# Turning half of the values back to front through DRAM instead of multiplying by reversed activations

## The chip, the cores and the metric

The kernel runs on one core of a Trainium2 chip. The metric is the device time of one execution in microseconds (us), taken as the median over several runs. The engines are named as the profile names them: PE is TensorE (matrix products, with PEld for loading the stationary operand), DVE is VectorE, ACT is ScalarE, POOL is GpSimd, SP is SyncE. ACT, POOL and SP can start DMA transfers; an issue is listed as ACTq, POOLq or SPq.

## The reference, cut to what matters

Two decoder layers act on 256 tokens of width 2048, all in float32. The change lies in the first mixer of the first layer, in its second half, a gated linear recurrence of eight heads of width 128 called `hgrn2`:

```python
def mixer_ab(h, w_in, ...):
    u, v, q, f, i, g = jnp.split(h @ w_in, cuts, axis=-1)     # each 256 x 1024
    ...
    y_b = hgrn2(q, f, i, g, lower_bound, o_gain)

def hgrn2(q, f_logit, i, g, lower_bound, o_gain):
    ...
    k = (1.0 - lb) * jax.nn.sigmoid(-fl)
    vc = chunks(i)                                            # the values
    ...
        o_intra = jnp.einsum('bhts,bhsv->bhtv', scores, v_c)
        new_state = ... + jnp.einsum('bhsk,bhsv->bhkv', k_c * jnp.exp(G_end - G), v_c)
```

What is computed for the change is `i`, the values: the normalized input times a 2048 x 1024 matrix. The kernel sums over tokens in two blocks of 128, and it needs the second block of values with its tokens in reverse order (token 255 first).

## The kernel before

**Tiling.** Activations lie feature-major: 16 tiles `a` of 128 features, each with the high part and the low part of 256 tokens. Every weight piece is 128 x 1024 floats (512 KB). It goes through a fixed pipeline: SP issues its load into `w` (L195, five buffers), ACT rounds it to `wh` (L182, three buffers), DVE makes the rest `wl` (L183, three buffers), and PE multiplies with three products for each pair (high by high, high by low, low by high). PE reads a piece for about 2.6 us.

**Loops.** `project` makes one head's query from two pieces (L301). `project_tok` makes 512 columns of values for both token blocks from eight pieces (L325 to L327), with two accumulators, one for each block. `project_four` (L344 to L346) makes 512 gate columns. The loop over heads runs `project` for heads 0 to 7; `values` runs ahead of head 4 (values for heads 0 to 3) and ahead of head 7 (for heads 4 to 7). After head 7 comes `project_four` for the output gate.

**The reversed block before.** In `project_tok`, POOL copies both parts of each activation tile with the second block's tokens in reverse (L316, tile `ar`), and the second block's products use that copy as their stationary operand, so the values come out reversed. Each token's scale `Rt` has to be reversed too; the function `mirror` makes the reversed scales `Rr` on DVE, once. `values` then lets ACT scale both accumulators into `itok` (L798).

**Order of the work.** The recurrence of each head, `hgrn`, is a generator that is advanced one step by each `tick()`, that is, once for each weight piece. On ACT it copies decay levels (`E`, L729) that alternate with products on DVE (`kq`, L733), moves scores (`s128` L754, `st` L756, `s1` L765), and makes the next head's decay (`lf`, L695). On PE it makes the scores (L743, L751, L714) and the output (L773 to L775: `st0` and `s128` times the first block `itok[:, 0]`, `s1` times the reversed second block `itok[:, 1]`). The output step waits until `values` has entered its `itok` in the list `itoks` and two further ticks have passed. The framework's scheduler turns all of this into one fixed sequence for each engine. Every engine works its sequence from the front, and an instruction that waits holds up all behind it on that engine; that holds for a DMA issue too.

## Time and profile before

| | |
|---|---|
| median of 3 runs | 2175.03 us (2174.26 to 2176.19) |
| the profiled execution's own time | 2173.92 us |
| its span in the profile | 2172.1 us |
| PE busy | 2164.0 us, 100% of the span |
| DVE, ACT, POOL busy | 1601.1 us, 1313.6 us, 472.3 us |
| `project_tok` for the values | from 116 us to 184 us of the span |
| POOL's copies `ar<-a` | 32, together 19.6 us |

PE's work is fixed by the products, so the time is PE's busy time and the few microseconds in which PE waits. A change of anything else shows in the time only where it makes such a wait longer or shorter. The lines of the profile that carry this stand in the prediction.

### The profile page before, as it was taken

The numbers are of one execution on the slowest core, as the hardware profiler recorded it, in microseconds if no ns is written. First come the engines' busy times: TensorE is split into PE (matmuls) and PEld (weight loads), VectorE is DVE, ScalarE is ACT, GpSimd is POOL, SyncE is SP. The second block draws the span as 40 slices with busy tenths as digits, with TensorE's granted clock in tenths as the row PEclk, the third lists the DMA queues.
The fourth block names the chain that finished last, engine by engine and source line by source line (L and its number), as shares of the span: only waits on it lengthen the run. The fifth ranks groups of instructions, "written<-read, shape, count | busy, mean of one in ns | idle before, by whom it ended". The sixth has DMA issues, their size and how long they took to land.

```text
span 2172.1 us, 32509 instructions
## 1 busy us (share of the span) xinstructions
PE 2164.0 (100%) x10874; PEld 1900.8 (88%) x10874; DVE 1601.1 (74%) x2286; ACT 1313.6 (60%) x1951; POOL 472.3 (22%) x865
## 2 busy tenths in 40 slices
PE   9999999999999999999999999999999999999999
PEld 8988888888888888888888888888888888888888
DVE  7788768777567757776987887877777577667766
ACT  7678766665556545654666556666666466456642
POOL 1252221212012002111233443212211012011202
PEclk9999999999999999999999999999999999999999
DMA  8655677777676767776777766787777677666866
GB/s 311 209 160 177 209 238 222 240 233 236 210 228 206 235 209 219 226 237 206 241 230 229 238 207 209 221 246 222 230 227 242 198 232 217 228 215 204 251 212 192
DMA packets 492617, 483.55 MB, mean 223 GB/s; under 512 B 115137, under 2 KB 460369, under 8 KB 492321
## 3 DMA queue, kind: packets, MB, share of 16 engines
q1 hardware_dynamic: 465888, 453.27, 66.2%
q0 software_dynamic: 24832, 25.92, 5.1%
q10 hardware_dynamic: 1728, 2.28, 0.3%
q8 instruction: 85, 1.39, 0.3%
q14 instruction: 84, 0.68, 0.1%
HBM read 435.18 MB, written 2.11 MB: 201 GB/s over the span
## 4 chain that ended last, share of the span: by engine, by line
PE 94%; DVE 2%; ACT 2%; issue 1%; DMA 1%; POOL 0%; SPq 0%; ACTq 0%; DVEq 0%
PE pm L344 26%; PE pm L345 26%; PE pm L346 26%; PE pm L325 4%; PE pm L326 4%; PE pm L327 4%; PE pm L233 1%; PE pm L301 1%; ACT wh L182 1%; DVE wl L183 1%; DMA pt<-ptmp 1%; PE pm L257 1%; DVE kq L733 0%; ACT E L729 0%; DVE st L762 0%
## 5 line engine op out<-in xcount | busy, mean ns | idle before, releaser
L183 DVE TENSOR_TENSOR wl<-w,wh 128x1024 fp32r<-128x1024 f32 (+1 forms) x820 | 990.9, 1218 | 448.7 <-ACT wh L182 437.0
L182 ACT ACTIVATE wh<-w 128x1024 fp32r<-128x1024 f32 (+1 forms) x820 | 856.0, 1049 | 608.8 <-PE pm L346 447.7
L344 PE MATMUL pm<-wh,a 128*128 128x512 f32 x1728 | 655.9, 380 | 0.0
L345 PE MATMUL pm<-wl,a 128*128 128x512 f32 x1728 | 655.3, 379 | 0.3 <-DVE wl L183 0.3
L346 PE MATMUL pm<-wh,a 128*128 128x512 f32 x1728 | 654.9, 379 | 0.0
L364 POOL DMA_DIRECT2D zt<-tmp x413 | 223.5, 549 | 1134.6 <-DVE tmp L357 1022.6
L345 PEld LDWEIGHTS pm<-wl,a 128*128 128x128 f32 x1728 | 326.6, 189 | 47.4 <-DVE wl L183 1.4
L346 PEld LDWEIGHTS pm<-wh,a 128*128 128x128 f32 x1728 | 326.6, 189 | 46.2
L344 PEld LDWEIGHTS pm<-wh,a 128*128 128x128 f32 x1728 | 326.5, 189 | 46.2
L344 PE MATMUL pm<-wh,hid 128*128 128x512 f32 x688 | 260.8, 379 | 0.0
L345 PE MATMUL pm<-wl,hid 128*128 128x512 f32 x688 | 260.8, 379 | 0.0
L346 PE MATMUL pm<-wh,hid 128*128 128x512 f32 x688 | 260.8, 379 | 0.0
L326 PE MATMUL pm<-wl,a 128*128 128x512 f32 x416 | 158.1, 380 | 2.3 <-DVE wl L183 2.3
L325 PE MATMUL pm<-wh,a 128*128 128x512 f32 x416 | 158.7, 381 | 0.0
L327 PE MATMUL pm<-wh,a 128*128 128x512 f32 x416 | 157.8, 379 | 0.0
L345 PEld LDWEIGHTS pm<-wl,hid 128*128 128x128 f32 x688 | 130.0, 189 | 18.5
L346 PEld LDWEIGHTS pm<-wh,hid 128*128 128x128 f32 x688 | 130.0, 189 | 18.5
L344 PEld LDWEIGHTS pm<-wh,hid 128*128 128x128 f32 x688 | 130.0, 189 | 18.4
L1238 ACT ACTIVATE conv<-zt,pp 128x256 f32<-128x256 f32 x176 | 95.9, 590 | 70.6 <-DMA zt<-tmp 62.5
L364 POOL DMA_DIRECT2D turn<-tmp x160 | 86.9, 551 | 224.4 <-DVE tmp L357 129.6
L1239 DVE SCALAR_TENSOR_TENSOR conv<-zt,pp,conv 128x255 f32<-128x255 f32 x176 | 80.2, 479 | 54.4 <-ACT conv L1238 35.4
L357 DVE STREAM_TRANSPOSE tmp<-z 128x512 f32<-128x512 f32 x120 | 97.8, 851 | 7.1 <-ACT z L1224 5.1
(252 smaller groups left out, 2245.2 us busy)
## 6 DMA issues: line engine op xcount, KB each, us to landing
w<-in_w_up SPq DMA_DIRECT2D x352, 512.0 KB, 5.0
w<-in_w_dn SPq DMA_DIRECT2D x176, 512.0 KB, 5.0
w<-in_w_cqkv SPq DMA_DIRECT2D x96, 512.0 KB, 4.6
w<-in_w_abo SPq DMA_DIRECT2D x32, 512.0 KB, 4.9
w<-in_w_cg SPq DMA_DIRECT2D x32, 512.0 KB, 5.3
w<-in_w_co SPq DMA_DIRECT2D x32, 512.0 KB, 4.9
zt<-tmp SPq DMA_DIRECT2D x414, 32.0 KB, 2.6
zt<-tmp POOLq DMA_DIRECT2D x413, 32.0 KB, 2.4
```

The source lines that it names most:

```text
L182: r = deep["wh"] = SC.activation(wh, w, AF.Copy)
L183: deep["wl"] = V.tensor_tensor(wl, w, wh.bitcast(F32), ALU.subtract)
L325: PE.matmul(to_two(ps[T]), ah, h, start=k + i == 0, stop=False)
L326: PE.matmul(to_two(ps[T]), ah, l, start=False, stop=False)
L327: deep["last"] = PE.matmul(to_two(ps[T]), al, h, start=False, stop=k + i == KT - 1)
L344: PE.matmul(to_rows(ps[T]), ah, h, start=not begun and k + i == ks[0], stop=False)
L345: PE.matmul(to_rows(ps[T]), ah, l, start=False, stop=False)
L346: deep["mm"] = deep["last"] = PE.matmul(to_rows(ps[T]), al, h, start=False, stop=not more and k + i == ks[-1] + 1)
L357: V.transpose(tmp.rearrange("p (b m i t) -> p b m i t", b=4, m=4, t=2)[:, :, :, :, T], src(T).rearrange("p (m b j) -> p b m j", m=4, b=4))
L364: queues[(a + b) % len(queues)].dma_start(dst[BLK * b:BLK * (b + 1), :, a * n:(a + 1) * n], tmp[BLK * a:BLK * (a + 1), b * 4 * n:(b + 1) * ...
L1238: held(SC.activation(c, z, AF.Identity, bias=pp[:, cb:cb + 1], scale=w(2)))
L1239: V.scalar_tensor_tensor(c[:, 1:], z[:, :S - 1], w(1), c[:, 1:], ALU.mult, ALU.add)
```

## The change

The reversed copies on POOL, the reversed scales and the function `mirror` go. The second block's values come out in natural order. ACT scales them into a tile `late`, and a new generator `flip` takes them to `itok[:, 1]` by three DMAs, all issued on ACT: SBUF to a DRAM tile, that DRAM tile to a second one with the 128 rows read from the last to the first, and the second DRAM tile to SBUF. Each moves 256 KB (128 rows of 2 KB). `flip` issues one for each tick, and each needs the one before to have landed. `itoks` gets its entry when the third one is issued.

```diff
@@ mixes()
                 for m in both:
                     next(m, None)
                 yield
-            yield from mirror()
-
-        Rr = hp.tile([P, LANE], F32, tag="Rr", name="Rr")[:, 0:2]
-
-        def mirror():
-            yield
-            r = hp.tile([P, 512], F32, tag="junk", name=nm("junk"), bufs=1)
-            ra, rb = (r[:, i * BLK:(i + 1) * BLK] for i in range(2))
-            held(V.tensor_copy(ra, Rt[:, 1:2].to_broadcast([P, BLK])), "wl")
-            V.tensor_copy(Rr[:, 0:1], Rt[:, 0:1])
-            V.transpose(rb, ra)
-            V.transpose(ra, view(rb, BLK - 1, (-1, BLK)))
-            for a in range(4):
-                V.tensor_copy(Rr[BLK * (3 - a):BLK * (4 - a), 1:2], ra[BLK * a:BLK * (a + 1), 0:1])
@@ mixer_ab()
+        def flip(itok, late, r, f):
+            SC.dma_start(r, late)
+            yield
+            SC.dma_start(bass.AP(f.tensor, f.offset, [[S, 2], [512, P], [1, S]]),
+                         bass.AP(r.tensor, r.offset + (P - 1) * 512, [[S, 2], [-512, P], [1, S]]))
+            yield
+            SC.dma_start(itok[:, 1], f)
+            itoks.append((itok, steps[0]))
+
         def values(j):
-            ps = project_tok(w_i[j], norm, lambda: hp.tile([P, 512], F32R, tag="ar", name=nm("ar"), bufs=3))
+            ps = project_tok(w_i[j], norm)
             itok = hp.tile([P, 2, 512], F32, tag="tok", name=nm("itok"), bufs=2)
-            for T in range(2):
-                SC.activation(cols2(itok[:, T]), of_two(ps[T]), AF.Copy, scale=Rr[:, T:T + 1])
-            itoks.append((itok, steps[0]))
+            late = hp.tile([P, 512], F32, tag="ar", name=nm("late"), bufs=1)
+            SC.activation(cols2(late), of_two(ps[1]), AF.Copy, scale=Rt[:, 1:2])
+            SC.activation(cols2(itok[:, 0]), of_two(ps[0]), AF.Copy, scale=Rt[:, 0:1])
+            start(flip(itok, late, *rowsd[j]))
 
         silu = []
+        dp = es.enter_context(tc.tile_pool(name="da", bufs=1, space=bass.MemoryType.DRAM))
+        rowsd = [[dp.tile([P, 512], F32, tag=f"rd{i}{n}", name=f"rd{i}{n}") for n in range(2)] for i in range(2)]
...
             if h in (4, 7):
-                values(len(itoks))
+                values(h // 7)
```

The scheduler's sequences stay what they were except between the first `values` and the first pieces of the output gate, on PE, DVE, ACT and POOL; SP's sequence is the same. Three places of that stretch follow. The lines of the changed kernel are smaller by 15 there (L714 is L729 of before) and by 3 from `gated` on. The number at the end of a name is the program's own for that buffer, and it differs between the two kernels for the same piece.

First, ACT behind the first `values`. Before, both `itok` copies are followed by three weight pieces (`wh`) with the recurrence's work between them:

```order
L798 ACTIVATE itok_267_1644<-pm_218_1331,Rr_544 128x512
L798 ACTIVATE itok_267_1644<-pm_219_1332,Rr_544 128x512
L729 ACTIVATE E_252_1548<-kq_178_997 128x128 x2
L182 ACTIVATE wh_284_1785<-w_283_1784 128x1024
L754 ACTIVATE s128_271_1675<-px_270_1649 128x128
L756 ACTIVATE st1_974<-px_270_1649 64x64 x2
L695 ACTIVATE lf_206_1232<-lf_206_1232,gm_545 128x256
L182 ACTIVATE wh_289_1834<-w_288_1833 128x1024
L729 ACTIVATE E_277_1730<-kq_183_1033 128x128 x2
L182 ACTIVATE wh_297_1917<-w_296_1916 128x1024
L765 ACTIVATE s1_272_1684<-st1_974 128x128
```

The piece `wh_284` feeds the first half of head 5's query and `wh_289` its second half. In the changed kernel these two are `wh_275` and `wh_281`, and behind `itok`, `late` and one pair of `E` copies ACT's sequence is this:

```order
L780 DMA rd00_986<-late_259_1617 128x512
L739 ACTIVATE s128_263_1649<-px_262_1623 128x128
L741 ACTIVATE st1_973<-px_262_1623 64x64 x2
L182 ACTIVATE wh_275_1754<-w_274_1753 128x1024
L714 ACTIVATE E_269_1705<-kq_182_1029 128x128 x2
L680 ACTIVATE lf_205_1228<-lf_205_1228,gm_544 128x256
L782 DMA rd01_987<-rd00_986 2x128x256
L750 ACTIVATE s1_264_1658<-st1_973 128x128
L714 ACTIVATE E_269_1705<-kq_182_1029 128x128 x2
L836 ACTIVATE kq_206_1229<-pm_261_1622,gm_544 128x128 x2
L182 ACTIVATE wh_281_1810<-w_280_1809 128x1024
L785 DMA itok_258_1616<-rd01_987 128x512
```

The second half's piece, which stood ahead of the copy `s1`, now stands behind it, behind two pairs of copies and behind the second transfer; the third transfer follows it.

Second, PE in head 5's query, where the output step of head 0 stands. Before, the step stands ahead of that query, in one piece:

```order
L301 MATMUL pm_269_1648<-a_58_378,wh_279_1739 128x256 x2
L301 MATMUL pm_269_1648<-a_58_378,wl_280_1740 128x256
L773 MATMUL px_282_1771<-itok_267_1644,st0_973 128x128
L774 MATMUL px_282_1771<-itok_267_1644,s128_240_1486 128x128
L775 MATMUL px_282_1771<-itok_267_1644,s1_246_1511 128x128
L301 MATMUL pm_281_1770<-a_13_116,wh_284_1785 128x256 x2
L301 MATMUL pm_281_1770<-a_13_116,wl_285_1786 128x256
```

In the changed kernel it stands after the first half of the query, and its last product, which reads the reversed block, some rows further on:

```order
L301 MATMUL pm_273_1746<-a_38_256,wl_276_1755 128x256
L758 MATMUL px_277_1783<-itok_258_1616,st0_972 128x128
L759 MATMUL px_277_1783<-itok_258_1616,s128_240_1486 128x128
L301 MATMUL pm_273_1746<-a_39_290,wh_281_1810 128x256 x2
L301 MATMUL pm_273_1746<-a_39_290,wl_282_1811 128x256
L301 MATMUL pm_273_1746<-a_40_293,wh_281_1810 128x256 x2
L301 MATMUL pm_273_1746<-a_40_293,wl_282_1811 128x256
L301 MATMUL pm_273_1746<-a_44_315,wh_281_1810 128x256 x2
L760 MATMUL px_277_1783<-itok_258_1616,s1_241_1495 128x128
L301 MATMUL pm_273_1746<-a_44_315,wl_282_1811 128x256
```

PE's product L760 now waits for the third transfer, in the middle of the second half; the product L301 with `wl_282` ahead of it waits for that piece.

Third, ACT behind the second `values`, at the end of head 7's query. Before, the second piece of the output gate is `wh_375`:

```order
L182 ACTIVATE wh_370_2476<-w_369_2475 128x1024
L781 ACTIVATE px_355_2343,sos_972<-o_174_985,Rt_89_514 128x128
L729 ACTIVATE E_348_2310<-kq_221_1334 128x128 x2
L695 ACTIVATE lf_227_1373<-lf_227_1373,gm_545 128x256
L182 ACTIVATE wh_375_2507<-w_374_2506 128x1024
L99 ACTIVATE sos_972<-rm_359_2386 128x8
```

In the changed kernel that piece is `wh_360`. The second transfer (L782) stands two rows ahead of this excerpt:

```order
L714 ACTIVATE E_333_2265<-kq_220_1330 128x128
L99 ACTIVATE sos_971<-sos_971 128x8
L714 ACTIVATE E_333_2265<-kq_220_1330 128x128
L836 ACTIVATE kq_226_1367<-pm_339_2296,gm_544 128x128 x2
L739 ACTIVATE s128_352_2420<-px_351_2394 128x128
L714 ACTIVATE E_333_2265<-kq_220_1330 128x128 x2
L741 ACTIVATE st1_973<-px_351_2394 64x64
L785 DMA itok_337_2291<-rd11_989 128x512
L741 ACTIVATE st1_973<-px_351_2394 64x64
L680 ACTIVATE lf_225_1366<-lf_225_1366,gm_544 128x256
L182 ACTIVATE wh_360_2463<-w_359_2462 128x1024
L182 ACTIVATE wh_365_2501<-w_364_2500 128x1024
```

The piece `wh_360` now stands behind the copies `kq` (which read head 7's finished query), behind the next scores and behind the third transfer.

## The prediction

> **What bounds the kernel now.** I read the page's table of engines first, then the list of what PE waited for, then the stretch of the values in order of time.
>
> ```profile
> PE 2164.0 (100%) x10874; PEld 1900.8 (88%) x10874; DVE 1601.1 (74%) x2286; ACT 1313.6 (60%) x1951; POOL 472.3 (22%) x865
> ```
>
> PE is busy for 2164.0 of 2172.1 us. The change adds and removes no product, so those 2164.0 us stay. What can move is the time in which PE waits. The list of waits, for PE over the whole span (total, times, longest):
>
> ```profile
> PE pm L326 <- DVE wl L183: 2.3, 3, 1.3
> PE warm L149 <- DVE ones L85: 1.1, 1, 1.1
> PE pm L301 <- DVE wl L183: 0.6, 1, 0.6
> PE pm L345 <- DVE wl L183: 0.3, 1, 0.3
> ```
>
> PE waits 4.3 us in all, never for POOL's copies `ar`. The L326 and L301 waits, 2.9 us, lie in the stretch that is changed, and each is for a weight's rest `wl`. Two of them in order of time:
>
> ```profile
> 162.58 0.48 PE L326 MATMUL pm<-wl,a 128*128 128x512 f32 x1 [0.62 <-DVE wl L183]
> ```
>
> ```profile
> 185.24 0.38 PE L301 MATMUL pm<-a,wl 128*128 128x256 f32 x1 [0.58 <-DVE wl L183]
> ```
>
> So in this stretch ACT and DVE, which make `wh` and `wl` between the recurrence's work, are barely in time; what delays them there delays PE. Elsewhere the sequences are unchanged and PE hardly waits, so a delay made here is not won back.
>
> **What is removed.** POOL's copies:
>
> ```profile
> L316 POOL CAST ar<-a x32: 395/586/1447, 5.6 to 178.0; 128x256 fp32r<-128x256 f32 x32
> L183 DVE TENSOR_TENSOR wl<-w,wh x27: 1155/1225/1428, 121.2 to 204.1; 128x1024 fp32r<-128x1024 f32 x27
> ```
>
> PE never waited for them, so their 32 copies are worth nothing by themselves. They may have slowed DVE: in this stretch a `wl` took between 1.16 and 1.43 us. From 0 to 1.0 us of DVE's chain ahead of the first output step may come back (four slow products at 0.27 us); I take 0.3, one slow product, as the median 1.225 lies near the fast end. `mirror`'s eight small DVE instructions lie ahead of the values, where the list leaves at most L345's 0.3 us to win: nothing. The scalings of both accumulators stay two ACT copies: nothing. SP's sequence is unchanged.
>
> [...]
>
> **What is added: how long a transfer takes.** Three of 256 KB after each `values`. The nearest rows are, first, the weight loads `w` (512 KB into SBUF) while the values are computed, second, the stores of `out` (128 to 512 KB from SBUF to DRAM):
>
> ```profile
> DMA to landing us min/median/max: 3.4/3.8/5.2
> ```
>
> ```profile
> DMA to landing us min/median/max: 2.0/2.4/3.9
> ```
>
> A bounce through DRAM exists once, `cd`, written by POOL and read back as `cb`. The first line is POOL's wait for the write, the second the time of these transfers:
>
> ```profile
>   POOL cb L985: 4.7, 1
> ...
> DMA to landing us min/median/max: 3.7/5.3/8.3
> ```
>
> I take 2.4 us for the first (a store), 3.8 for the third (a load), and 4.7 for the second. No row shows DRAM to DRAM: it is bounded by 2.0 (the fastest store) and 8.3 (the slowest `cb`), and the bounce's wait is the row nearest to a read of what was just written.
>
> [...]
>
> ACT is not held while a transfer runs, only where the next one's issue stands ahead of unfinished work:
>
> ```profile
> 39.46 1.06 ACT L182 ACTIVATE wh<-w 128x1024 fp32r<-128x1024 f32 x1
> 39.46 0.33 ACTq L524 DMA_DIRECT2D wt<-in_spw  x1
> ```
>
> An issue can start together with the copy ahead of it.
>
> **First place: behind the first `values`.** ACT and DVE before:
>
> ```profile
> 141.73 0.51 ACT L729 ACTIVATE E<-kq 128x128 f32<-128x128 f32 x2
> 142.14 1.04 ACT L182 ACTIVATE wh<-w 128x1024 fp32r<-128x1024 f32 x1
> 143.09 0.25 ACT L754 ACTIVATE s<-px 128x128 f32<-128x128 f32 x1
> 143.25 0.43 ACT L756 ACTIVATE st<-px 64x64 f32<-64x64 f32 x2
> 143.71 0.60 ACT L695 ACTIVATE lf<-lf,gm 128x256 f32<-128x256 f32 x1
> ...
> 148.82 0.31 ACT L765 ACTIVATE s<-st 128x128 f32<-128x128 f32 x1 [1.60 <-DVE st L762]
> 149.04 0.49 ACT L729 ACTIVATE E<-kq 128x128 f32<-128x128 f32 x2
> 149.56 0.62 ACT L839 ACTIVATE kq<-pm,gm 128x128 f32<-128x128 f32 x2
> ```
>
> ```profile
> 143.42 0.32 DVE L722 TENSOR_TENSOR kq<-kq,lf 128x128 f32<-128x128 f32 x1
> 143.65 1.20 DVE L183 TENSOR_TENSOR wl<-w,wh 128x1024 fp32r<-128x1024 f32 x1
> 144.89 0.45 DVE L762 COPY_PREDICATED st<-msk,lv 128x128 f32<-128x128 uint16 x1
> 145.14 0.50 DVE L733 TENSOR_TENSOR kq<-kq,lf 128x256 f32<-128x256 f32 x1
> 145.53 0.28 DVE L762 COPY_PREDICATED st<-msk,lv 128x128 f32<-128x128 uint16 x1
> 145.72 0.94 DVE L699 RECIPROCAL kd<-lf 128x128 f32<-128x128 f32 x1
> ```
>
> I put these durations into the new sequence; neighbours overlap by about 0.1, as the starts show. The first transfer goes out at 142.0 and lands at 144.4. ACT makes `s128` and `st`, then head 5's first `wh` by 143.8, the `E` pair once DVE has finished its `kq` product (144.4), and `lf`. It reaches the second transfer at 145.0, later than 144.4, so that wait is hidden by ACT's own work.
>
> The copy `s1` waits for five mask copies on DVE. After L722, DVE's new order is two of them with a `kq` product between (to 144.5), `wl` (145.7), mask copy, product, mask copy (146.5), reciprocal (147.4), last mask copy (147.65). Then ACT: `s1` and `E` to 148.5, the two `kq` copies to 149.0, and only now `wh` for head 5's second half, to 150.0; its `wl` ends at 151.25. When PE needs them:
>
> ```profile
> 148.94 0.39 PE L301 MATMUL pm<-a,wh 128*128 128x256 f32 x2
> ...
> 149.61 0.39 PE L301 MATMUL pm<-a,wh 128*128 128x256 f32 x2
> ```
>
> PE starts that half at 148.94 and reads `wl` 0.22 later, so it waits to 151.25: 2.1 us, whatever the transfers do. L760 stands after the pair at 149.61, at 149.83, thus at 151.9 after that wait. The third transfer goes out when ACT has dispatched that `wh` (149.0) and the second has landed (145.0 + 4.7 = 149.7); it lands at 153.5. PE passes there 153.5 - 149.8 = 3.7 us late. Bounds: 2.1 (the piece alone, transfers at 2.0) and 9.5 (3.9, 8.3 and 5.2: 142.0 + 3.9, + 8.3, + 5.2 = 159.4).
>
> What is late next: behind L760, ACT waits with head 0's output copy; the weights for head 5's end and head 6 are dispatched or ready by then, so nothing more.
>
> **Second place: behind the second `values`.** PE before:
>
> ```profile
> 190.37 0.28 PE L301 MATMUL pm<-a,wl 128*128 128x256 f32 x1
> ...
> 191.18 0.33 PE L751 MATMUL px<-E 128*32 128x64 f32 x7
> ...
> 194.13 0.38 PE L344 MATMUL pm<-wh,a 128*128 128x512 f32 x1
> ```
>
> The gate's second piece was rounded ahead of all this; now ACT does it after `kq`, which reads the query that ends at 190.65, and after `s128`, which reads the scores that end at 191.51. From there 0.25 (`s128`), 0.51 (`E`), 0.43 (`st`), 0.60 (`lf`), less overlaps: `lf` ends near 193.1, `wh` near 194.1. DVE's reciprocal (0.94, after `lf`), a mask copy and `wl` end near 195.35, and PE wants that `wl` at 194.35: 1.0 us. The third transfer's wait adds nothing as long as the second lands by 192.2: it goes out near 187.6, and 187.6 + 4.7 = 192.3. At 8.3 us it adds 3.7. The output step that reads this block comes later than the landing.
>
> **The sum.** +3.7 and +1.0. The two waits shown above, 0.62 and 0.58, lie behind the first place; PE then is 3.7 us later while ACT and DVE go on, so I count both as gone: -1.2. DVE's gain: -0.3. Together +3.2 us on the profiled execution's 2173.92, that is 2177.1; that execution lies 1.1 below the median 2175.03, so the median becomes 2178.2 us, +0.15%. The bounds give +0.9 (2.1 + 1.0 - 1.2 - 1.0) and, with both transfer bounds, +13.
>
> **The rivals.** (1) Slow transfers: the second at 6 to 8.3 us and the third at 5.2, among weight loads. For it speak the `cb` row; against it, that stores took 2.4. At 6 the first place costs 145.0 + 6 + 5.2 - 149.8 = 6.4 and the second 1.0 + 1.4; less 1.2 the median is near 2182.5, up to 2188. (2) Not slower: the waits of 2.9 us before come from POOL's copies holding up DVE, and without them ACT runs ahead. It decides from the point where ACT dispatches head 5's second `wh` 2.1 us earlier, so that PE finds its `wl`, and the third transfer with it lands by 149.8. Then PE loses nothing here and gains up to 2.9: 2172.1 to 2175. Against it: `s1` waits for DVE's last mask copy, which is behind a reciprocal that has nothing to do with POOL; and a third transfer dispatched at 146.9 needs 2.9 us to land. (3) ACT held at the transfers' issues itself: if the store takes 5 us, ACT stands at the second transfer until 147.0, still ahead of the 147.65 at which `s1` can start; so it costs nothing below 5.6 us, and above that 1 us for each. [...]
>
> **Chances.** Forecast 0.62 (+0.9 to +6), slow transfers 0.23, not slower 0.11, ACT held 0.04. A measurement of this kernel tells about 0.2%, 4.35 us, from no change. Of the forecast's 0.62, 0.30 lies beyond that bound, since the transfers' prices spread upward; the rest and nearly all of rival 2 lie within it: slower 0.56, same 0.41. Faster by 0.2% would need all 4.3 us of PE's waits to go: 0.03. The range 2175.3 to 2184.5 leaves out the lower part of rival 2 and the upper part of rival 1.
>
> **What would show it.** In the changed kernel's list of waits, PE L760 waits about 1.6 us for the DMA into `itok`, and PE L301 about 2 us for `wl` just ahead of it; an L345 wait for `wl` of about 1 us stands near 197; the waits at L326 and L301 near 162 and 185 are gone. The times from issue to landing on ACT's queue give the three prices. PE's busy time stays at 2164 us. I am wrong if PE waits in this stretch no more than before, or if the second transfer took far from 4.7 us.

## The result, and the profile after

The changed kernel takes 2196.62 us (median of 5 runs, 2195.70 to 2198.09) against 2175.03 us (5 runs beside them, 2174.10 to 2176.20). The ratio is 1.010, with a 95% interval of 1.0085 to 1.0114: 21.6 us slower. The forecast was 3.2 us slower, and its range ended at 2184.5.

The profiled execution took 2195.70 us with a span of 2193.7. The page's line of engines, which answers to the one quoted of before:

```profile
PE 2170.1 (99%) x10874; PEld 1903.7 (87%) x10874; DVE 1598.2 (73%) x2278; ACT 1314.5 (60%) x1951; POOL 453.6 (21%) x833
```

The same 10874 products keep PE busy 6.1 us longer. The rest of the span's 21.6 us is waiting. What PE waited for (total, times, longest):

```profile
PE pm L344 <- ACT wh L182: 8.1, 1, 8.1
PE px L760 <- DMA itok<-rd: 4.7, 1, 4.7
PE pm L301 <- ACT wh L182: 1.8, 1, 1.8
PE pm L301 <- DVE wl L183: 1.7, 3, 0.8
PE pm L345 <- DVE wl L183: 1.2, 3, 0.5
PE warm L149 <- DVE ones L85: 1.1, 1, 1.1
PE pm L326 <- DVE wl L183: 1.0, 2, 0.8
```

Two single waits stand out. The longer one, 8.1 us, is for no transfer at all: it is for a rounded weight piece `wh` from ACT. ACT in order of time, first behind the first `values`, then behind the second (ACTq rows are the issues of the transfers; in brackets the idle time before an instruction and what ended it):

```profile
146.72 1.22 ACTq L782 DMA_DIRECT2D rd<-rd  x1
...
149.28 1.05 ACT L182 ACTIVATE wh<-w 128x1024 fp32r<-128x1024 f32 x1
155.32 0.33 ACTq L785 DMA_DIRECT2D itok<-rd  x1
155.70 0.51 ACT L714 ACTIVATE E<-kq 128x128 f32<-128x128 f32 x2 [5.36 <-DMA rd<-rd]
...
200.47 0.60 ACTq L782 DMA_DIRECT2D rd<-rd  x1
201.17 0.21 ACT L99 ACTIVATE sos<-rm 128x8 f32<-128x8 f32 x1 [1.84 <-DMA rd<-late]
...
202.86 0.20 ACT L741 ACTIVATE st<-px 64x64 f32<-64x64 f32 x1
208.96 0.32 ACTq L785 DMA_DIRECT2D itok<-rd  x1
209.33 0.22 ACT L741 ACTIVATE st<-px 64x64 f32<-64x64 f32 x1 [6.27 <-DMA rd<-rd]
209.57 0.60 ACT L680 ACTIVATE lf<-lf,gm 128x256 f32<-128x256 f32 x1
210.08 1.99 ACT L182 ACTIVATE wh<-w 128x1024 fp32r<-128x1024 f32 x2
```

The issue of the third transfer waits for the second to land, and ACT's whole sequence stands behind that issue, for 5.36 and 6.27 us. Behind it stand, among others, the next pieces `wh`. In the second place ACT had also stood at the second transfer's issue, 1.84 us, until the store landed. What came of it on PE:

```profile
157.96 0.80 PE L760 MATMUL px<-itok,s 128*128 128x128 f32 x2 [4.66 <-DMA itok<-rd]
...
211.17 1.22 PE L344 MATMUL pm<-wh,a 128*128 128x512 f32 x2 [8.12 <-ACT wh L182]
```

In the second place ACT's two idle times, 1.84 and 6.27 us, add up to 8.11, and PE's wait is 8.12.

The second transfer lasts from its issue to the next one's, 146.72 to 155.32 and 200.47 to 208.96: 8.6 and 8.5 us. The store took 5.3 us and the load 2.6 by the table of DMA issues (its last column is the median time from issue to landing):

```profile
rd<-late ACTq DMA_DIRECT2D x2, 256.0 KB, 5.3
...
itok<-rd ACTq DMA_DIRECT2D x2, 256.0 KB, 2.6
```

The table by stretches of 2 us around the second wait (busy time of PE, PEld, DVE, ACT, POOL, then the granted TensorE clock with 1.00 as full speed, the DMA engines' share, GB/s):

```profile
202.00:204.00 2.00, 1.05 (x5) 0.57 (x3) 1.93 (x7) 1.06 (x6) 0.00 (x0) 1.00 0.48 161
204.00:206.00 2.00, 0.00 (x0) 0.00 (x0) 0.22 (x2) 0.00 (x0) 0.00 (x0) 0.97 0.14 48
206.00:208.00 2.00, 0.00 (x0) 0.00 (x0) 0.00 (x0) 0.00 (x0) 0.00 (x0) 0.50 0.14 48
...
214.00:216.00 2.00, 2.00 (x6) 1.60 (x5) 1.21 (x2) 0.83 (x2) 1.91 (x3) 0.50 0.85 268
216.00:218.00 2.00, 2.00 (x27) 1.70 (x27) 0.25 (x2) 1.15 (x2) 0.34 (x1) 0.97 0.88 233
```

Two things are to be seen. Between 204 and 208 us the second transfer is alone, and the sixteen DMA engines are busy for 0.14 of the time, which is close to two engines of sixteen (0.125). And the granted clock falls to 0.50 about 3 us after PE stops at 203.05 and is back only some 5 us after it resumes at 211.17. In the first place it is 0.50 from about 151 to 161 us. A product of 512 columns takes 0.63 us at that clock in place of 0.38; that is where most of PE's 6.1 us more of busy time come from.

So the first theory had a chain of four links. The second transfer's pattern has an outermost length of 2 and keeps about two of the sixteen DMA engines busy (0.14); so it takes 8.5 us; so ACT is held; so PE waits and then runs at half clock. The experiments take the links one by one. Theory A in their expectations is that the outermost length of 2 is the cause; theory B is that reading rows backwards is.

### The profile page after: what moved, and what is told of

It reads as the page before. It is cut to its first block, busy times and chain, and to the rows that moved or that the text cites. A ratio compares the mean times of both kernels' runs of the same rounds, so it can differ in the third digit from the quotient of the medians.

```text
span 2193.7 us, 32471 instructions
## 1 busy us (share of the span) xinstructions
PE 2170.1 (99%) x10874; PEld 1903.7 (87%) x10874; DVE 1598.2 (73%) x2278; ACT 1314.5 (60%) x1951; POOL 453.6 (21%) x833
## 4 chain that ended last, share of the span: by engine, by line
PE 87%; DVE 4%; DMA 4%; ACT 2%; issue 1%; SPq 1%; POOL 0%; DVEq 0%; ACTq 0%
PE pm L345 24%; PE pm L346 24%; PE pm L344 24%; PE pm L325 4%; PE pm L327 4%; PE pm L326 4%; DVE wl L183 1%; PE pm L233 1%; DMA w<-in_w_up 1%; ACT wh L182 1%; DMA rd<-rd 1%; PE pm L301 1%; DMA pt<-ptmp 1%; PE pm L257 0%; SPq L364 0%
## 5 line engine op out<-in xcount | busy, mean ns | idle before, releaser
L344 PE MATMUL pm<-wh,a 128*128 128x512 f32 x1728 | 656.8, 380 | 8.1 <-ACT wh L182 8.1
L345 PE MATMUL pm<-wl,a 128*128 128x512 f32 x1728 | 656.3, 380 | 1.3 <-DVE wl L183 1.2
L346 PE MATMUL pm<-wh,a 128*128 128x512 f32 x1728 | 655.7, 379 | 0.0
L344 PEld LDWEIGHTS pm<-wh,a 128*128 128x128 f32 x1728 | 327.0, 189 | 54.7 <-ACT wh L182 8.5
L344 PE MATMUL pm<-wh,hid 128*128 128x512 f32 x688 | 260.8, 379 | 0.0
L326 PE MATMUL pm<-wl,a 128*128 128x512 f32 x448 | 170.2, 380 | 1.0 <-DVE wl L183 1.0
L325 PE MATMUL pm<-wh,a 128*128 128x512 f32 x448 | 170.8, 381 | 0.3 <-ACT a L382 0.3
L327 PE MATMUL pm<-wh,a 128*128 128x512 f32 x448 | 169.9, 379 | 0.0
L344 PEld LDWEIGHTS pm<-wh,hid 128*128 128x128 f32 x688 | 130.0, 189 | 18.5
```

The costliest lines, as they stand in the source:

```text
L325: PE.matmul(to_two(ps[T]), ah, h, start=k + i == 0, stop=False)
L326: PE.matmul(to_two(ps[T]), ah, l, start=False, stop=False)
L327: deep["last"] = PE.matmul(to_two(ps[T]), al, h, start=False, stop=k + i == KT - 1)
L344: PE.matmul(to_rows(ps[T]), ah, h, start=not begun and k + i == ks[0], stop=False)
L345: PE.matmul(to_rows(ps[T]), ah, l, start=False, stop=False)
L346: deep["mm"] = deep["last"] = PE.matmul(to_rows(ps[T]), al, h, start=False, stop=not more and k + i == ks[-1] + 1)
```

## The experiments: what makes the second transfer slow

**x_forward** reads the rows in natural order, in the same shape.

```diff
-                         bass.AP(r.tensor, r.offset + (P - 1) * 512, [[S, 2], [-512, P], [1, S]]))
+                         bass.AP(r.tensor, r.offset, [[S, 2], [512, P], [1, S]]))
```

> The middle transfer copies the rows in their own order instead of from the last to the first; its shape (two half rows outside, 128 rows inside) stays. The second block of values stays in natural order, so the output step gets wrong values; all work and all waits are there. Theory A (the transfer is slow because its outermost dimension has length 2, so few DMA engines work on it): it still takes 8.5 us and the time stays near 2196. Rival B (reading the rows backward is what is slow): about 3 us, and the time falls to about 2179. Rival C (DRAM to DRAM is slow as such): 8.5 us, like A.

Measured: 2196.22 us, ratio 1.0095 (1.0074 to 1.0115); the second transfer takes 8.8 and 8.4 us. The direction costs nothing, and theory B falls.

**x_four** cuts the rows into four columns of 512 bytes instead of two of 1024; **x_thin** into sixteen of 128 bytes.

```diff
-            SC.dma_start(bass.AP(f.tensor, f.offset, [[S, 2], [512, P], [1, S]]),
-                         bass.AP(r.tensor, r.offset + (P - 1) * 512, [[S, 2], [-512, P], [1, S]]))
+            SC.dma_start(bass.AP(f.tensor, f.offset, [[P, 4], [512, P], [1, P]]),
+                         bass.AP(r.tensor, r.offset + (P - 1) * 512, [[P, 4], [-512, P], [1, P]]))
```

In x_thin the lists are `[[32, 16], [512, P], [1, 32]]` and `[[32, 16], [-512, P], [1, 32]]`.

> The middle transfer has four quarter rows (512 bytes) outside and 128 rows, last to first, inside. Theory A: its data part, 8.5 less about 2 us for what any transfer takes, halves: about 5.3 us; PE's wait at L760 falls from 4.7 to about 1.5 and the one at L344 from 8.1 to about 5; about 2186 us. Rivals B and C: 8.5 us, about 2196.

> The middle transfer of the kernel after with an outermost dimension of 16 and runs of 128 bytes instead of 2 and 1024 bytes. If the outermost length alone sets the time (16 of them spread over all DMA engines), it takes 4 us or less and the time is like the split's, 2181 to 2186. If the length of the runs counts as much (four outermost with 512 bytes took 6.3 and 7.8 us, little under the 8.5 of two with 1024), it takes 8 us or more and the time is 2195 or more.

Measured: x_four 2191.76 us, ratio 1.0074 (1.0057 to 1.0091), the transfer 6.3 and 7.8 us, slower than expected. (For the 2 us that the expectation takes for any transfer, the nearest rows are those of 32 KB in the kernel after: 1.7 us at the least, 1.9 to 3.1 us by their medians.) x_thin 2188.52 us, ratio 1.0061 (1.0041 to 1.0081), the transfer 4.2 and 4.3 us from issue to issue. While it runs all but alone in x_thin, the DMA engines' share is near 1, as this stretch shows:

```profile
200.00:201.00 1.00, 0.00 (x0) 0.00 (x0) 1.00 (x2) 0.20 (x2) 0.00 (x0) 1.00 0.98 153
```

In x_four the last four microseconds of the second place's transfer show 0.11 to 0.27. Runs of 128 bytes are slow here for each engine (153 GB/s at a share of 0.98, where the kernel after moves 48 at 0.14), but with all sixteen at work the transfer takes half of what it took with an outermost length of 2 (4.2 and 4.3 us against 8.6 and 8.5). Among these three patterns the outermost length decides, and the length of the runs matters far less. The shares are 0.14, up to 0.27, and 0.98 for 2, 4 and 16 outermost; 2, 4 and 16 engines of sixteen would be 0.125, 0.25 and 1. x_thin's time missed its expected 2181 to 2186; a faster second transfer alone does not make the kernel fast. As this transfer too goes from DRAM to DRAM, rival C of x_forward (slow as such) falls with it.

**x_split** turns the rows in two steps, each with a positive outermost step: the store reverses the rows within groups of 16, and the second transfer swaps the eight groups, sixteen rows outermost, whole rows of 2 KB.

```diff
-            SC.dma_start(r, late)
+            SC.dma_start(bass.AP(r.tensor, r.offset + 15 * 512, [[16 * 512, 8], [-512, 16], [1, 512]]), late)
...
-            SC.dma_start(bass.AP(f.tensor, f.offset, [[S, 2], [512, P], [1, S]]),
-                         bass.AP(r.tensor, r.offset + (P - 1) * 512, [[S, 2], [-512, P], [1, S]]))
+            SC.dma_start(bass.AP(f.tensor, f.offset, [[512, 16], [16 * 512, 8], [1, 512]]),
+                         bass.AP(r.tensor, r.offset + 7 * 16 * 512, [[512, 16], [-16 * 512, 8], [1, 512]]))
```

> The order is reversed in two steps, with long outermost dimensions: the store reverses the rows within groups of 16, the middle transfer has 16 rows outside and eight groups, last to first, inside, each a whole row of 2 KB. Theory A: the middle transfer takes about 3 us, the store stays near 5 us or, with an outer dimension of 8 instead of 128, gets 1 us longer; the waits fall to about 2 us at the first place (for the weight's piece) and 1 us at the second; about 2179 us, what was forecast. Rivals B and C: 8.5 us, about 2196.

Measured: 2183.64 us, ratio 1.0035 (1.0022 to 1.0048), the second transfer 4.0 us in both places. 13 of the 21.6 us are gone, less than expected. It is 4.9 us below x_thin, whose second transfer is nearly as fast; why was not tried. What is left on PE:

```profile
PE pm L344 <- ACT wh L182: 3.7, 1, 3.7
PE pm L345 <- DVE wl L183: 1.4, 4, 0.6
...
PE pm L301 <- ACT wh L182: 1.0, 1, 1.0
```

PE no longer waits for `itok` at all; it waits for ACT, which is still held for 1.1 and 1.9 us at the third issue and, in the second place, for 1.7 us at the second one, until the store lands (1.7 and 1.9 make 3.6 of PE's 3.7 us). PE's busy time is 2168.8 us, 4.8 more than before, most of it from the lower clock.

**x_natural** has no transfers; ACT scales both blocks into `itok` in natural order.

```diff
-            late = hp.tile([P, 512], F32, tag="ar", name=nm("late"), bufs=1)
-            SC.activation(cols2(late), of_two(ps[1]), AF.Copy, scale=Rt[:, 1:2])
+            SC.activation(cols2(itok[:, 1]), of_two(ps[1]), AF.Copy, scale=Rt[:, 1:2])
...
-            start(flip(itok, late, *rowsd[j]))
+            itoks.append((itok, steps[0]))
```

> The changed kernel without the three transfers: ACT scales the second block straight into the output step's tile, in natural order, so the output step gets wrong values. It shows what the removal of the reversed copies and scales is worth alone. Theory: POOL's copies cost DVE little; 0 to 1 us faster than the kernel before. Rival: the 2.9 us of PE's waits in this stretch came from them: about 2172 us.

Measured: 2174.03 us, ratio 0.9994 (0.9985 to 1.0003) to 2175.43 us of before. What the change removes, POOL's 32 copies and `mirror`, is worth nothing that can be measured. All 21 us come from what it adds.

## The experiments: the lower clock by itself

**x_warm** fills PE's two waits with products of a zero tile, so that PE is hardly idle there. The order of all else is that of the kernel after.

```diff
+            for _ in range(34 if h == 0 else 0):
+                tied(PE.matmul(op[0:BLK, P:S], zero, i0, start=False, stop=False))
             tied(PE.matmul(op[:, P:S], s1, i1, start=False, stop=True))
@@ project_four(..., fill=32 for the first output gate)
+            for _ in range(fill if k == 2 else 0):
+                PE.matmul(ps[0][0:BLK, 0:P], zero, ones, start=False, stop=False)
```

> The kernel after with products of a zero tile put into TensorE's two waits (34 between the second and the third product of the first output step, 32 ahead of the second pair of w_g's products; they add zeros), some 0.22 us each, 7 us in each place; the order of everything else is the same. Theory D (the lower granted clock, 0.5 for some 8 us in each place, makes the products behind the waits slow, and costs about 6 us by itself): the clock stays at or near 1.0, the products behind the waits take 0.38 us and not 0.63, the transfers land as before, and the time is 4 to 7 us less than the kernel after: 2190 to 2193. Rival (the products behind the wait are slow because their weights come late, or the transfers' end decides everything): no gain, 2195 to 2199.

Measured: 2192.62 us, ratio 1.0081 (1.0064 to 1.0098), 4.0 us less than the kernel after, at the near end of what theory D expected. Two stretches of the second place:

```profile
204.00:206.00 2.00, 2.00 (x21) 2.00 (x19) 0.00 (x0) 0.00 (x0) 0.00 (x0) 1.00 0.14 49
212.00:214.00 2.00, 1.82 (x12) 1.49 (x10) 1.34 (x3) 1.72 (x3) 1.84 (x4) 1.00 0.88 276
```

The transfer runs as before (share 0.14), and the clock stays at 1.00 through and behind the wait. So 4.0 us of the 21.6 come back when the clock stays up; they are lost after the wait is over. In the second place of the kernel after, the fall to 0.50 came some 3 us after the last product and the return 4.9 us after the next one. In the first place the fall, at about 151.3 us, came although PE had worked for 0.5 us between its waits of 1.78 and 0.77 us. In x_split, waits of 1.0 and 0.8 us were enough in the first place:

```profile
150.00:152.00 2.00, 1.49 (x8) 1.49 (x9) 0.88 (x2) 1.70 (x5) 0.82 (x2) 0.70 0.54 152
152.00:154.00 2.00, 2.00 (x11) 2.00 (x11) 2.00 (x3) 1.87 (x6) 0.29 (x1) 0.50 0.68 250
```

So the fall also came here with no single wait longer than 1.0 us, when two stood close together.

## The experiments: who is held

**x_pool** issues the three unchanged transfers on POOL; **x_both** does so with the split's shapes. Each `SC.dma_start` in `flip` becomes `nc.gpsimd.dma_start`:

```diff
-            SC.dma_start(itok[:, 1], f)
+            nc.gpsimd.dma_start(itok[:, 1], f)
```

> The three transfers are issued on GpSimd's queue instead of ScalarE's; their shapes stay. In the kernel after, ScalarE's two idle times of 5.4 and 6.3 us end with the middle transfer, because the third transfer's issue waits for it on ScalarE and the halves of the weights (L182) are queued behind. Theory A1 (the hold on ScalarE is what carries the second place, the late value itself only the first): the middle transfer still takes 8 to 9 us, the wait of 8.1 us of TensorE for ScalarE's weights in the second place is gone, ScalarE has no idle time that ends with the middle transfer, the first place keeps a wait of TensorE for itok of 4 to 8 us: 2182 to 2188. Rival A2 (the late value carries both places, whoever issues): the second place waits as long, now for itok: 2194 or more. Rival A3 (GpSimd's queue is slower or is itself held, and its turns of other tiles come late): over 2197.

> The split reversal of the earlier run (store reverses within 16 rows, middle transfer swaps the 8 groups, 16 rows outermost) and the issue on GpSimd's queue together. The split alone has a middle transfer of 4.0 us, was about 8 us slower than the kernel before, and its longest wait is 3.7 us of TensorE for ScalarE's weights in the second place, behind ScalarE's 1.9 us hold. If the length of the middle transfer and the hold on ScalarE are the whole cause, both are gone: the wait of 3.7 us and the lower clock behind it vanish, the first place waits for itok 0 to 3 us: 2175 to 2179. If the rest of the split's loss has another source (three more transfers on the DMA engines, the later output step as such), it stays: 2182 or more.

Measured: x_pool 2206.43 us, ratio 1.0140 (1.0125 to 1.0156), outside what A1 expected and in the range of A3, that POOL's queue is itself held. The scheduler had put the second `values`' store ahead of the first `values`' load in POOL's sequence, so the load waited for a store that could not start before 179.6 us. The groups of the store and of the load, with their shortest, median and longest time in ns and the first and last start:

```profile
L780 POOL DMA_DIRECT2D rd<-late x2: 602/603/604, 141.4 to 179.6; - x2
...
L785 POOL DMA_DIRECT2D itok<-rd x2: 593/601/609, 183.5 to 209.5; - x2
```

This run tells nothing of the hold; it shows that a queue's written order can be worse than the hold. x_both has the loads in place and took 2192.17 us, ratio 1.0077 (1.0062 to 1.0092), against 2183.64 for the same shapes on ACT. That is not the 2175 to 2179 of the first case, but the "2182 or more" of another source. ACT is free there, and PE waits for the landing:

```profile
PE px L760 <- DMA itok<-rd: 12.1, 2, 6.5
```

From POOL the store took 5.1, the second 4.9 and the load 4.7 us from issue to landing (medians). In the first place that is 16 us from the store's issue at 141.3 to L760 at 157.5. Issued on ACT, the load took 2.5.

**x_two** has two hops: the store of the split, then eight loads of 16 rows, 32 KB each, in reverse order of the groups, all on ACT.

```diff
+            for g in range(8):
+                SC.dma_start(itok[16 * g:16 * (g + 1), 1], r[16 * (7 - g):16 * (8 - g)])
```

> Two hops instead of three: the store reverses the rows within groups of 16, and eight loads of 16 rows, 32 KB each, fetch the groups in reverse order; no transfer from DRAM to DRAM; everything on ScalarE's queue. In the split with three hops the chain was 5.1 us for the store, 4.0 for the middle, 2.5 for the load, and the first place gives about 7 us between the late values and the product that reads them. If the length of the chain against these 7 us and the hold on ScalarE for the middle transfer decide, the chain becomes 5.1 + 2.4 + eight issues of 0.3 = some 10 us, nothing on ScalarE waits for a middle transfer, the wait of 3.7 us in the second place is gone: 2177 to 2181. If eight issues hold ScalarE as long as the one wait did, or the store alone (over 4.8 us in every run) is enough to hold it: 2182 to 2186.

Measured: 2191.02 us, ratio 1.0070 (1.0055 to 1.0085), worse than both cases expected. ACT behind the second `values`:

```profile
199.03 3.61 ACTq L783 DMA_DIRECT2D itok<-rd  x8
202.75 0.21 ACT L99 ACTIVATE sos<-rm 128x8 f32<-128x8 f32 x1 [5.09 <-DMA itok<-rd]
```

Eight issues of 0.45 us keep ACT's sequence for 3.6 us, on top of the wait for the store, and PE waits 5.4 us for `wh`. Issuing holds ACT as waiting does.

**x_gate** is the split on ACT with the output step two ticks later.

```diff
-            itoks.append((itok, steps[0]))
+            itoks.append((itok, steps[0] + 2))
```

> The split on ScalarE's queue, with the output step allowed two ticks later (entry in itoks plus 2); the transfers and their places on ScalarE's queue stay. Theory A (two separate costs: the product that reads the late value in the first place, ScalarE's hold in the second): the first place gets 1 to 3 us shorter, the second keeps its wait of some 3.7 us for ScalarE's weights: 2180 to 2183. If the late read is all, 2176 to 2178; if the later output step only moves the wait to the heads behind it, 2184 or more.

Measured: 2185.67 us, ratio 1.0045 (1.0028 to 1.0062), no better than the split's 2183.64, and in the range in which the later step only moves the wait. (There are four tables `st`; with the delay, head 4 writes head 0's before head 0's step has read it, so that step works with other weights in x_gate, x_sp_gate and x_sp_gate3. The instructions are the same in number and size.) With ACT still held, 4.3 us at L344 and 1.6 at L301 both for `wh`, more time for the landing buys nothing.

**x_sp** puts the split's three transfers on SP's queue, **x_sp_plain** the unchanged ones. Each `SC.dma_start` in `flip` becomes `nc.sync.dma_start`:

```diff
-            SC.dma_start(itok[:, 1], f)
+            nc.sync.dma_start(itok[:, 1], f)
```

> The split with its three transfers issued on SyncE's queue, where the loads of the weights stand, in place of ScalarE's. ScalarE has then no hold; on GpSimd's queue the same split took 16 us from the first issue to the landing of the load and TensorE waited 12.1 us for it in two places. If the landing time is what counts and SyncE's queue reaches the transfers as early as ScalarE's did: first place 0 to 4 us, second 0 to 2, 2177 to 2181. If SyncE comes to them late, or its loads of weights are held behind the waits for the store and the middle transfer, weights come late and the time is 2185 or more.

> The transfers of the kernel after, unchanged in shape, on SyncE's queue: the hold on ScalarE alone is taken away, the middle transfer keeps its 8.5 us. Theory A (two causes): the second place's wait of 8.1 us for ScalarE's weights goes, and the chain of 5.3 + 8.5 + 2.6 to 5 us, some 4.5 longer than in the split on SyncE's queue (2177.8 us, with waits of 2.6 and 1.9 us at the output steps), makes the waits at the output steps in both places 4 to 5 us longer each, with the lower clock behind them 2 to 3 us more: 2185 to 2191. If the hold was nearly all, 2178 to 2182. If the length of the transfer was nearly all, 2194 or more.

Measured: x_sp 2177.79 us, ratio 1.0013 (1.0003 to 1.0022). x_sp_plain 2180.06 us, ratio 1.0021 (1.0012 to 1.0031), better than theory A's 2185 to 2191. The second transfer there still takes over 8 us:

```profile
196.89 0.61 SPq L782 DMA_DIRECT2D rd<-rd  x1
197.60 4.58 SPq L195 DMA_DIRECT2D w<-in_w_g  x2
205.06 0.34 SPq L785 DMA_DIRECT2D itok<-rd  x1
```

So 16.6 of the 21.6 us went by changing the queue, with the slow transfer kept. SP is held too: nothing is issued from 150.46 us to the third transfer at 155.20, nor from 202.18 to the other at 205.06. But its loads of weights run ahead of their use, and PE's list of waits names no load. (Of the waits that the expectation of x_sp_plain puts at the output steps, the 2.6 us stand at L699, a product of the scores.)

Two cautions, as the scheduler orders the work anew for each kernel. It put ACT's weight pieces back where they stood before the change: in the first place of x_sp_plain three of them start at 142.39, 144.46 and 146.42 us, ahead of `s1` at 149.07. So the run takes away the hold and ACT's changed order together. And it moved L760 further back: by the trace 8 products stand between L759 and L760 in the kernel after, 113 in x_sp and 209 in x_sp_plain, so there PE has other work until the landing.

**x_hold** takes the reader away. It keeps every transfer and every wait on ACT, but nothing reads what lands.

```diff
-            SC.dma_start(itok[:, 1], f)
+            SC.dma_start(late, f)
...
+            SC.activation(cols2(itok[:, 1]), of_two(ps[1]), AF.Copy, scale=Rt[:, 1:2])
```

> The kernel after with all its transfers and waits on ScalarE, but nothing reads what they bring: the third transfer loads back into the buffer of the late values, and ScalarE also writes the second block straight into itok, in natural order (two more activations of 0.69 us; the output step gets it unreversed, so its values are not the reference's). The order on TensorE differs from the kernel after only in the product of the late values, some five products earlier. If the hold on ScalarE is nearly all of the 21 us: TensorE's waits for ScalarE's weights stay (1.8 and 8.1 us in after), in the first place grow by what the wait for itok hid, and the time is 2190 to 2197. If the read of the landed values is the larger part: the wait of 4.7 us for itok and its lower clock go, 2181 to 2187.

Measured: 2198.61 us, ratio 1.0106 (1.0089 to 1.0123), as slow as the kernel after, and 1.6 us above the range for the hold as nearly the whole cause. PE's waits, the product that ends the first of them, and ACT's third issue with the first piece behind it:

```profile
PE pm L301 <- ACT wh L182: 9.6, 1, 9.6
PE pm L344 <- ACT wh L182: 9.2, 1, 9.2
...
159.61 0.80 PE L301 MATMUL pm<-a,wh 128*128 128x256 f32 x2 [9.58 <-ACT wh L182]
...
156.36 0.32 ACTq L785 DMA_DIRECT2D late<-rd  x1
...
158.52 1.04 ACT L182 ACTIVATE wh<-w 128x1024 fp32r<-128x1024 f32 x1
```

With no reader the wait at L760 is gone, and the next product waits for `wh` instead. So the loss needs no reader of the late value: the hold on ACT can make all of it. In the first place it is not quite the same hold, though. The piece for the second half of head 5's query starts at 158.52 us, behind the third issue; in the kernel after it starts at 149.28, ahead of it, and the next two pieces behind the issue start at 156.32 and 157.66. How long PE would have waited there for these, had L760 not waited 4.7 us for the landing, no run shows.

In the second place ACT's order from the second issue on is that of the kernel after, and there the traces settle it. With the transfers on ACT, PE's wait at L344 is the sum of ACT's two idle times at the issues: 8.11 (sum) and 8.12 us (wait) in the kernel after, 8.57 and 8.59 in x_forward, 7.77 and 7.79 in x_four, 4.44 and 4.47 in x_thin, 3.60 and 3.68 in x_split, 8.99 and 9.17 here; in x_gate, 3.98 and 4.34. ACT's changed order by itself costs little there; the wait is the hold.

**x_sp_gate**, **x_sp_gate3** and **x_sp_late** take the hold and the early read away: the split on SP's queue, with the output step two ticks later. The second has three buffers for `s1`; the third has five tables `st` as well, so that each step finds its own.

```diff
+            itoks.append((itok, steps[0] + 2))
...
-        sts = [hp.tile([P, 2, P], F32, tag=f"st{i}", name=f"st{i}") for i in range(4)]
+        sts = [hp.tile([P, 2, P], F32, tag=f"st{i}", name=f"st{i}") for i in range(5)]
...
-            st = sts[h % 4]
+            st = sts[h % 5]
...
-            s1 = hp.tile([P, P], F32, tag="s1", name=nm("s1"), bufs=2)
+            s1 = hp.tile([P, P], F32, tag="s1", name=nm("s1"), bufs=3)
```

> The same on SyncE's queue with the output step two ticks later. If the landing time against the output step is all that is left, both places are free: 2174 to 2177, no slower than the kernel before. If SyncE's hold on the weights is the cost, as long as without the later step: 2182 or more.

> The split on SyncE's queue with the output step two ticks later and three buffers (two before) for the step's last table, s1, so that a head does not overwrite a table that the delayed step has yet to read. If the transfers' landing time against the output step and the hold are the whole cause, nothing is left: within 0.1% of the kernel before, 2174 to 2177.5. If something else that the transfers bring (their load on the DMA engines, the later output step) costs time, 2179 or more. Faster than before by over 0.2% is expected by neither: with no transfer at all the kernel took 2174.0.

> The split on SyncE's queue, the output step two ticks later, with five tables st and three tables s1 where the kernel after has four and two, so that the delayed step still finds its own head's. If hold and landing are the whole cause: within 0.1% of the kernel before, 2173.5 to 2177.5, as with four tables (2174.7 and 2175.4). If a further cost hides in the tables: 2179 or more.

Measured: 2175.44 us, 1.0000 (0.9991 to 1.0009); 2174.70 us, 0.9996 (0.9987 to 1.0005); 2175.01 us, 1.0000 (0.9990 to 1.0009). Nothing is left of the loss; PE's longest wait in x_sp_late is 1.7 us, at L760. It ties with the kernel before and cannot well beat it, since the kernel with no transfer at all took 2174.03.

| second transfer, median in us | issued on ACT | issued on SP | SP, output step later |
|---|---|---|---|
| outermost length 2, 8.5 us | 2196.62 | 2180.06 | |
| outermost length 16, 4.0 us | 2183.64 | 2177.79 | 2175.01 |
| none | 2174.03 | | |

## Why the prediction was wrong

The direction was right, the size was not: 21.6 us against 3.2. By its own steps:

- **What is removed.** "Worth nothing by themselves" for POOL's copies, and 0.3 us for DVE: right, by x_natural (between 0.15% faster and 0.03% slower). The spread of `wl`, which the prediction thought the copies might have made, stays without them: 1.16 to 1.43 us before and 1.16 to 1.51 after, from 120 to 215 us.
- **The price of the second transfer failed.** It was put at 4.7 us, with 8.3 as the upper bound; it took 8.5 to 8.6. The step took the bounce's wait as "the row nearest to a read of what was just written" and never looked at the transfer's own shape, an outermost length of 2, though the order quoted in the change prints it as `2x128x256`. No row of before shows what that length costs; the runs do: 8.5 us for 2, 6.3 and 7.8 for 4, 4.2 and 4.3 for 16. A second transfer far from 4.7 us is a sign of being wrong that the prediction itself had named. The store was low too: 2.4 taken, 5.3 and 4.2 measured. The load was high: 3.8 against 2.6.
- **The first place.** The wait for `wl` ahead of L760 was forecast at 2.1 us and came as 1.78 for `wh` and 0.77 for `wl`: near in size, and right in cause: the piece started at 149.28, and 149.0 was forecast. With the measured prices the same working lands the third transfer at 142.0 + 5.3 + 8.6 + 2.6 = 158.5, which is 8.7 us behind 149.8 in place of 3.7; the three waits sum to 7.2.
- **The second place.** "The third transfer's wait adds nothing as long as the second lands by 192.2: [...] At 8.3 us it adds 3.7." The mechanism was seen and dismissed through the price. With 8.5 us and a store 1.8 us longer it gives 1.0 + 3.9 + 1.8 = 6.7; measured 8.1, all of it ACT standing at the two issues.
- **"So nothing more" behind L760** held for the waits: PE's next one comes at 194.00. That is in part luck. The hold delayed the next pieces too, to 156.32 and later, and L760's wait stood in front of that. Where a piece that PE needs stands behind such a hold, as in x_hold, PE waits 9.6 us.
- **ACT held** got a chance of 0.04, priced at the second transfer's issue behind the store. In the first place that was right: the issue stood until 146.72, and `s1`, the next copy on ACT, waited until 148.03 for DVE. In the second place the same issue cost 1.84 us, and most of the hold sat one transfer later, at the third issue behind the second. That an issue which waits holds the engine that issues it now has its rows: ACT's idle times of 1.84, 5.36 and 6.27 us.
- **PE's busy time "stays at 2164 us"** was wrong: 2170.1, for the most part from the lower clock. The prediction had no term for that.
- **The relief of 1.2 us** came about in part: the wait of 0.62 at 162.58 is gone, and of the 0.58 at 185.24 there is 0.30 left, at 194.00. The rest of L326's fall from 2.3 to 1.0 lies ahead of the first place, at about 133 and 136 us (1.69 before, 0.95 after); this fits DVE's gain, put at 0.3.

Put together, the prediction's working with measured prices gives 8.7 + 6.7 - 1.2 - 0.3 = 13.9 us. PE's longer busy time adds 6.1, which makes 20.0 of the 21.6. What is left is the balance of small differences, 1.4 us more in the second place and 1.5 less in the first among them. So the steps that failed are the price of the second transfer, the hold on ACT that follows from it, and the missing term for the clock. Rival 1, slow transfers, was the right one in kind, but its 2182.5, up to 2188, lacked the clock and used the same short store.

## What to carry to other kernels

A transfer that depends on another costs its wait on the queue that issues it, and everything behind it on that engine pays (here 5.36 and 6.27 us on ACT): read from the trace what stands behind the issue, and give a chain of transfers to a queue whose work runs ahead of its use (here SP: 2180.1 instead of 2196.6, with nothing else in the kernel's text changed, though the scheduler's order changed with it). On the engine that is held, add up its idle times at the issues: in the second place their sum was PE's wait. Price a transfer by its own pattern, not by the nearest one of the same bytes: an outermost length of 2 made 256 KB take 8.5 us, one of 16 took 4.0. And when a forecast makes PE wait, add the time that it may then run at half clock: it came in this stretch after each single wait of 3.7 us or more whose products the traces show (3.68 us in x_split, 4.47 in x_thin, 5.42 in x_two, 5.54 and 6.53 in x_both, 8.12 in the kernel after, 9.58 in x_hold), and in x_split after waits of 1.0 and 0.8 us close together. PE's busy time grew by 6.1 us for two places, 4.0 of which filling the waits gave back.

## What was not expected of the hardware

- One transfer from DRAM to DRAM with an outermost length of 2 moved 48 GB/s at an engine share of 0.14, alone on the chip's core. Sixteen outermost took about half the time even in pieces of 128 bytes (4.2 and 4.3 us against 8.6 and 8.5).
- The granted clock fell to 0.50 within a single wait of 3.7 us (x_split), at about 198.6 us, and came back at about 205.4, though PE had resumed at 199.7 (mean of 0.65 from 198 to 200 and of 0.64 from 204 to 206). In x_split PE's busy time grew by 4.8 us, most of it from the lower clock, beside waits of 3.7, 1.0 and 0.8 us: what followed the waits lost nearly as much as they did. How long a wait must be for the fall, the runs don't show: a wait of 2.65 us at L699 was followed by it in x_sp (about 157.1 to 160.5 us), one of 2.57 us was not in x_sp_plain, and in x_split waits of 1.0 and 0.8 us were.
- A store of 256 KB took 3.5 to 5.9 us in all versions, mostly twice what the stores of `out` took (2.4). Why was not tried; weight loads ran beside it (in the kernel after five were issued from 140.94 to 160.53 us, around the store of 141.37).
- The same load took 2.4 to 3.4 us issued on ACT, 3.4 to 5.3 on POOL and 3.1 to 5.6 on SP. On SP it shares its queue with the weight loads; whether that makes it longer, and what does on POOL, the runs don't show.
